# The FFN's down projection as seven products of half-size blocks

## The chip, the cores and the metric

The kernel runs on one core of one Trainium2 chip. The metric is the device time of one execution in microseconds (us). The kernel before takes 1400.53 us in the median of three runs (1400.05 to 1403.93).

## The reference, cut to what matters

One layer: a token mixer (projections, gated delta rule, pooling, output projection) and then a gated ConvFFN. All of it is float32; D is 1024, there are 1024 tokens, and D_FF is 2816, which is 22 groups of 128 channels.

```python
def conv_glu_ffn(h, w_up, conv_w, w_down):
    gate, up = jnp.split(h @ w_up, 2, axis=-1)
    return (jax.nn.silu(depthwise_conv(gate, conv_w)) * up) @ w_down

x = x + gt1 * rms_norm(yx, g_post_mix)
hx = rms_norm(x, g_pre_ffn) * (1 + sc2) + sh2
x = x + gt2 * rms_norm(conv_glu_ffn(hx, w_up, conv_ffn, w_down), g_post_ffn)
```

The change touches the last product, (1024 tokens x 2816 channels) times (2816 x 1024), and what feeds it and follows it.

## The kernel before

Every large product is made of three matmuls: each float32 operand is split into a high part (a cast on ScalarE, ACT) and a low part (a subtraction on VectorE, DVE), and high x high, high x low and low x high are summed in PSUM. A matmul is 128 x 128 weights against 512 columns.

**The up projection** (`stream_up`, `up_out`, `prep`, `stream_split`) goes by one level of Strassen's algorithm already. For each of the 22 channel groups f there are seven products of 12 matmuls each, in the order 1, 6, 2, 7, 5, 4, 3. They use three PSUM pools: `pa` and `pb` with two banks each, `pc` with four. The sums of weight blocks (tile `a`) are made on POOL; the sums of the token blocks were made once, in `stream_T`. `up_out` takes a product out of its bank; products 2, 7, 4 and 3 add onto a bank that an earlier product left, and wait until that one has been taken out (`NEEDS`). Most of that is DVE work (`graw`, `upx`), some is ACT copies (`t`).

**The gate** (`gate(f)`) follows each group: one scaling and two multiply-adds on DVE for the convolution, SiLU on ACT, a multiplication on DVE, and a store of the 128 x 1024 result into DRAM (`gd[f]`). Its buffer is row 6 or 7 of the tile `hf` (eight rows of 1024), by turns.

**The down projection** takes the groups in chunks: (0, 1), then five chunks of four. `stream_down_prep` loads each group's gate output and its rows of w_down back in halves (tile `dst`, eight buffers), and splits them into tiles `opg` and `opd`, 88 halves in all. There are 14 slots for these tiles (`SLOT`): they become free one after another as the products of the last up group (f = 21) end, and later as chunks end (`hs`). `stream_down` runs over a chunk's eight token tiles t and two column halves g: 12 matmuls into one `pc` bank (6 for the first chunk), and `down_out` copies (first chunk, ACT) or adds (DVE) the bank onto row t of `hf`.

**The last norm** is in `down_out` and `finish`, for the last chunk only: sum of squares on ACT, multiplication by a gain on POOL, then on DVE the root (Newton steps on tiny tiles) and the residual sum into `x1o`, and two stores per token tile.

All loads and stores are issued from SyncE (SP), in one queue in order. The order of instructions comes from a planner in the kernel (`Streams`, `Clock`): generators are spawned with a priority (a smaller number goes first), and `yield` of an event's name waits in the plan. On top of it the framework moves instructions forward where they find their engine free; it keeps the data dependencies and the buffers.

Of the kernel before, what the change touches and what calls it, by code (L numbers as in the profile page):

```python
# [9 lines left out]
F32 = mybir.dt.float32  # L10
# [7 lines left out]
P = 128  # L18
# [109 lines left out]
class Streams:  # L128
# [10 lines left out]
    def signal(self, name):  # L139
        self.events[name] = max(self.now, self.clock.end)  # L140
# [42 lines left out]
def kernel(ctx: ExitStack, tc: tile.TileContext, I, out):  # L183
# [68 lines left out]
    def pc(shape):  # L252
        return psC.tile(shape, F32, name="pc", tag="pc")
# [5 lines left out]
    def split_steps(dst_hi, dst_lo, src, eng=V, copy=S.copy):  # L259
        copy(dst_hi, src)  # L260
        yield (dst_hi,)
        eng.tensor_tensor(dst_lo, src, dst_hi.bitcast(F32), ALU.subtract)
        yield (dst_hi, dst_lo)
# [1203 lines left out]
    SEQ += [(f, p) for f in range(2, NF) for p in (1, 6, 2, 7, 5, 4, 3) if f > 2 or p > 2]  # L1467
    NWQ, NST = 4, 8
    half = (slice(0, 512), slice(512, 1024))
    A, wq, up, bank = {}, {}, {}, {}  # L1470
    gd = dram.tile([NF, P, T], F32, name="gd")

    def st(name):
        return fa.tile([P, 4, P], F32, name=name, tag="st", bufs=NST)

    def prep(f):

        if f:
            yield f"pre{f - 1}"
        if f == 2:  # L1480
            yield "FT"
            w = fT.tile([P, 4, 512], F32, name="a2", tag="ht", bufs=10)
            for n in range(2):
                A[f, n + 1] = w[:, n].rearrange("p (k n) -> p k n", n=P)
                dma(out=A[f, n + 1], in_=I["w_up_t"][f][:, 4 * n:4 * n + 4])
            signal("a2")
            yield (w,)
            signal("A21")
            signal("A22")
        yield "st", 4  # L1490
        src = {"11": I["w_up_t"][f][:, 0:4], "12": I["w_up_t"][f][:, 4:8],
               "21": I["w_up_t"][NF + f][:, 0:4], "22": I["w_up_t"][NF + f][:, 4:8]}
        q = {}
        for n in ("11", "21", "22", "12"):
            q[n] = st("a" + n)
            dma(out=q[n], in_=src[n])
        signal(f"pre{f}")
        if f != 2:
            A[f, 1], A[f, 2] = q["11"], q["12"]
        yield (q["11"],)  # L1500
        if f != 2:
            signal(f"A{f}1")
        yield (q["21"], q["22"])
        G.tensor_tensor(q["22"], q["21"], q["22"], ALU.add)
# [24 lines left out]
        yield (A[f, 4],)  # L1529
        signal(f"A{f}4")  # L1530
# [127 lines left out]
    def gate(f):  # L1658
        yield "TD"
        yield f"E{f}4"  # L1660
        cw = sm[:, SM_FCONV + 3 * f:SM_FCONV + 3 * f + 3]
        rw, u, sg = up[f, "g"], up[f, "u"], W["hf"][:, 6 + f % 2, :]
        V.tensor_scalar(sg, rw[:, 0:T], cw[:, 0:1], None, ALU.mult)
        yield
        V.scalar_tensor_tensor(sg, rw[:, 1:T + 1], cw[:, 1:2], sg, ALU.mult, ALU.add)
        yield
        V.scalar_tensor_tensor(sg, rw[:, 2:T + 2], cw[:, 2:3], sg, ALU.mult, ALU.add)
        yield
        S.activation(sg, sg, AF.Silu)
        yield  # L1670
        V.tensor_tensor(sg, u[:, 0:T], sg, ALU.mult)
        yield
        dma(out=gd[f], in_=sg)
        signal(f"g{f}")
        yield


    CHUNKS = [(0, 1)] + [tuple(range(f, f + 4)) for f in range(2, NF, 4)]
    SLOT = [("ha", 1), ("ha", 1), ("ht", 6), ("ht", 6), ("ha", 2), ("ha", 2), ("ht", 7), ("ht", 7), ("ht", 5), ("ht", 5),
            ("ht", 4), ("ht", 4), ("ht", 3), ("ht", 3)]  # L1680
    ops, outs = {}, {}

    def stream_down_prep():
        n = 0
        for f in range(NF):
            yield f"g{f}"
            for x in "gd":
                tag, p = SLOT[n % 14]
                if n < 14:
                    yield f"D{p}"  # L1690
                else:
                    yield "hs", 1
                n += 1
                o = (h2p if tag == "ha" else fT).tile([P, 2, T], F32R, name="op" + x, tag=tag, bufs=4 if tag == "ha" else 10)
                ops[f, x] = o
                for h in half:
                    yield "st", 1
                    w = st("dst").rearrange("p k n -> p (k n)")
                    dma(out=w, in_=gd[f][:, h] if x == "g" else I["w_down"][f * P:(f + 1) * P, h])
                    yield (w,)  # L1700
                    yield from split_steps(o[:, 0, h], o[:, 1, h], w)
                    free("st", 1)
            signal(f"d{f}")

    def stream_down():
        for fs in CHUNKS:
            last = fs[-1] == NF - 1
            for t in range(NT):
                ts = slice(t * P, (t + 1) * P)
                ps = [pc([P, 512]) for _ in range(2)]  # L1710
                for g in range(2):
                    for ff in fs:
                        yield f"d{ff}"
                        a, b = ops[ff, "g"], ops[ff, "d"]
                        for i, (y, z) in enumerate(((0, 0), (0, 1), (1, 0))):
                            TE.matmul(ps[g], lhsT=a[:, y, ts], rhs=b[:, z, half[g]], start=(ff == fs[0] and i == 0),
                                      stop=(ff == fs[-1] and i == 2))
                        yield ()
                    spawn(down_out(fs, t, g, ps[g]), 1)
            free("hs", 2 * len(fs))  # L1720

    def down_out(fs, t, g, ps):
        yield (ps,)
        if fs[0] == 0:
            yield f"g{NF - 1}"
        av = W["hf"][:, t, half[g]]
        if fs[0] == 0:
            S.copy(av, ps)
        else:
            V.tensor_tensor(av, ps, av, ALU.add)  # L1730
        yield
        if g == 0 and fs[-1] == NF - 1:
            signal(f"e{t}")
        if fs[-1] < NF - 1:
            return
        if "gg2" not in W:
            W["gg2"] = [fa.tile([P, 512], F32, name="gg2", tag="wqh", bufs=NWQ) for _ in range(2)]
            for i in range(2):
                dma(out=W["gg2"][i], in_=ggd[1, 4 * i:4 * i + 4].rearrange("k p -> (k p)").partition_broadcast(P))
        if t not in outs:  # L1740
            outs[t] = gu("x1o")[:, 0:D]
            dma(out=outs[t], in_=x1d[t])
            outs[t, "s"] = outs[t - 1, "s"] if t % 2 and t < NT - 1 else (
                small.tile([P, 2, 2], F32, name="oss", bufs=3), small.tile([P, 2], F32, name="ors", bufs=3))
        ss = outs[t, "s"][0][:, t % 2 if t < NT - 2 else 0]
        jk = fT.tile([P, 512], F32, name="t1", bufs=2)
        S.activation(jk, av, AF.Square, accum_out=ss[:, g:g + 1])
        yield
        G.tensor_tensor(av, av, W["gg2"][g], ALU.mult)
        yield  # L1750
        signal(f"o{t}{g}")
        if g:
            fin.append(t)
            if t % 2 or t == NT - 2:
                spawn(finish(tuple(fin)), 1)
                fin.clear()

    fin = []

    def finish(tiles):  # L1760

        n = len(tiles)
        yield f"o{tiles[-1]}0"
        if tiles[-1] < NT - 1:
            yield f"e{tiles[-1] + 1}"
        ss, rs = outs[tiles[0], "s"]
        sv = ss[:, 0:n, 0]
        V.tensor_tensor(sv, sv, ss[:, 0:n, 1], ALU.add)
        V.tensor_scalar(sv, sv, 1.0 / D, EPS, ALU.mult, ALU.add)
        rsqrt(rs[:, 0:n], sv, n)  # L1770
        yield
        for j, t in enumerate(tiles):
            for h in half:
                V.scalar_tensor_tensor(outs[t][:, h], W["hf"][:, t, h], rs[:, j:j + 1], outs[t][:, h], ALU.mult, ALU.add)
                dma(out=out[t * P:(t + 1) * P, h], in_=outs[t][:, h])
                yield
# [100 lines left out]
```

## Time and profile before

| | us |
|---|---|
| median of three runs | 1400.53 |
| the profiled execution | 1400.56 |
| its span, first to last instruction | 1398.8 |
| PE busy (matmuls) | 1306.9 |
| DVE busy | 932.3 |
| ACT busy | 593.1 |
| POOL busy | 326.9 |
| down projection on PE, first to last matmul | 1141.73 to 1386.32 |

A busy PE says that some matmul is in the pipeline; one matmul is recorded with 393 ns while the next starts after some 231 ns, so rates are taken from chains of many matmuls. The token mixer fills the time until about 700 us, the up projection then runs until 1141.7, and the down projection until 1386.3; what follows is the last norm.

### The profile page before, as it was taken

How to read it: one execution, taken by the hardware profiler on the slowest of the kernel's cores; microseconds unless marked ns; L12 is line 12 of the kernel's file. 1: busy time of each engine (PE TensorE's matmuls, PEld its weight loads, DVE VectorE, ACT ScalarE, POOL GpSimd, SP SyncE). 2: the span in 40 equal slices, each digit the busy share in tenths (PEclk: the TensorE clock that was granted, in tenths of full speed). 3: DMA queues.
4: the chain of work that ended last, by engine and by line, in shares of the span. 5: the costliest groups of instructions: out<-in, count | busy, mean ns of one | idle time of the engine just before them, and what ended most of it. 6: DMA issues, size and time to landing. Idle time of an engine off the chain costs nothing.

```text
span 1398.8 us, 23797 instructions
## 1 busy us (share of the span) xinstructions
PE 1306.9 (93%) x8787; PEld 1026.9 (73%) x8787; DVE 932.3 (67%) x1922; ACT 593.1 (42%) x1424; POOL 326.9 (23%) x431
## 2 busy tenths in 40 slices
PE   6788989989999899879989999999999999999996
PEld 2456767777878688658767888888888887888885
DVE  1877656657688797478798776777666693533547
ACT  3555865457575354335452333333323362210212
POOL 0552425041322300030132332333223200000024
PEclk9989999999999999999989999999999999999998
DMA  9514665545452333664213322223222364312204
GB/s 343 186 37 130 179 191 139 162 113 183 140 171 58 105 92 89 192 211 151 82 56 111 107 91 90 90 99 106 85 89 90 106 229 178 121 38 83 91 24 158
DMA packets 129460, 174.63 MB, mean 125 GB/s; under 512 B 51680, under 2 KB 64832, under 8 KB 129344
## 3 DMA queue, kind: packets, MB, share of 16 engines
q1 hardware_dynamic: 128912, 172.70, 38.1%
q8 instruction: 69, 1.13, 0.3%
q10 hardware_dynamic: 432, 0.42, 0.1%
q14 instruction: 47, 0.39, 0.1%
HBM read 135.93 MB, written 37.14 MB: 124 GB/s over the span
## 4 chain that ended last, share of the span: by engine, by line
PE 72%; DVE 13%; DMA 6%; ACT 3%; issue 3%; POOL 2%; SPq 0%; DVEq 0%; ACTq 0%; POOLq 0%
PE pc L123 30%; PE pa L123 23%; PE pb L123 19%; DMA w_m<-in_wmod 2%; DVE hf L123 1%; DMA wo_st<-in_w_out 1%; DVE rs_a L123 1%; DMA w_mod<-in_wmod 1%; DVE x L123 1%; POOL stmp L123 1%; DVE gtmp L123 1%; POOL sX L123 1%; DVE wql L123 1%; DVE yrs L123 1%; DMA dst<-in_w_down 1%
## 5 line engine op out<-in xcount | busy, mean ns | idle before, releaser
L123 PE MATMUL pc<-opd,opg 128*128 128x512 f32 x1056 | 244.4, 393 | 0.1
L123 PEld LDWEIGHTS pc<-opd,opg 128*128 128x128 f32 x1056 | 198.0, 188 | 46.4 <-ACT hf L123 0.6
L123 POOL TENSOR_TENSOR a<-a,a 128x512 f32<-128x512 f32 x88 | 131.8, 1499 | 350.8 <-DMA a<-in_w_up_t 223.5
L123 ACT CAST wqh<-a 128x512 fp32r<-128x512 f32 x132 | 81.8, 621 | 237.3 <-PE pa L123 66.3
L123 PE MATMUL pa<-h_hi,w_hi 128*128 128x512 f32 x320 | 137.8, 431 | 2.5 <-ACT jk L123 1.2
L123 PE MATMUL pa<-h_hi,w_lo 128*128 128x512 f32 x320 | 128.7, 402 | 1.6 <-DVE w_lo L123 1.6
L123 PE MATMUL pa<-h_lo,w_hi 128*128 128x512 f32 x320 | 129.3, 404 | 0.0
L123 DVE TENSOR_TENSOR hf<-pc,hf 128x512 f32<-128x512 f32 x80 | 55.0, 688 | 104.3 <-PE pc L123 104.2
L123 DVE TENSOR_TENSOR wql<-a,wqh 128x512 fp32r<-128x512 f32 x132 | 109.6, 832 | 8.4 <-ACT wqh L123 8.4
L123 ACT CAST opg<-dst 128x512 fp32r<-128x512 f32 x44 | 26.2, 621 | 142.0 <-PE pc L123 70.9
L123 POOL TENSOR_TENSOR hf<-hf,gg 128x512 f32<-128x512 f32 x16 | 22.0, 1379 | 249.0 <-ACT t L123 249.0
L123 PEld LDWEIGHTS pa<-h_hi,w_hi 128*128 128x128 f32 x320 | 60.8, 190 | 15.7 <-issue 2.6
L123 PEld LDWEIGHTS pa<-h_hi,w_lo 128*128 128x128 f32 x320 | 60.4, 189 | 13.9 <-DVE w_lo L123 1.8
L123 DVE SCALAR_TENSOR_TENSOR cv<-raw,sm,cv 128x1024 f32<-128x1024 f32 x48 | 62.2, 1297 | 11.2 <-ACT cv L123 10.7
L123 PEld LDWEIGHTS pa<-h_lo,w_hi 128*128 128x128 f32 x320 | 60.8, 190 | 9.3 <-issue 1.8
L123 DVE SCALAR_TENSOR_TENSOR hf<-graw,sm,hf 128x1024 f32<-128x1024 f32 x44 | 56.7, 1290 | 0.7
L123 DVE TENSOR_TENSOR upx<-pb,t 128x512 f32<-128x512 f32 x44 | 30.4, 690 | 38.9 <-PE pb L123 38.6
L123 ACT ACTIVATE ws<-pc,btg 128x128 f32<-128x128 f32 x80 | 26.9, 367 | 46.1 <-PE pc L123 45.7
L123 DVE TENSOR_TENSOR w_lo<-w_st,w_hi 128x512 fp32r<-128x512 f32 x40 | 28.6, 717 | 26.4 <-ACT w_hi L123 16.5
L123 PE MATMUL pc<-wo_h,mxl 128*128 128x512 f32 x112 | 44.8, 400 | 0.6 <-DVE mxl L123 0.6
L123 PE MATMUL pc<-wo_h,mxh 128*128 128x512 f32 x112 | 44.8, 401 | 0.2 <-ACT mxh L123 0.2
L123 PE MATMUL pc<-wo_l,mxh 128*128 128x512 f32 x112 | 44.5, 400 | 0.0
(378 smaller groups left out, 3236.1 us busy)
## 6 DMA issues: line engine op xcount, KB each, us to landing
a<-in_w_up_t SPq DMA_DIRECT2D x90, 256.0 KB, 2.8
w_m<-in_wmod SPq DMA_DIRECT2D x64, 256.0 KB, 3.4
gd<-hf SPq DMA_DIRECT2D x22, 512.0 KB, 2.7
dst<-gd SPq DMA_DIRECT2D x44, 256.0 KB, 3.9
dst<-in_w_down SPq DMA_DIRECT2D x44, 256.0 KB, 4.2
w_st<-in_w_in_t SPq DMA_DIRECT2D x40, 256.0 KB, 3.4
w_mod<-in_wmod SPq DMA_DIRECT2D x16, 512.0 KB, 7.5
st<-in_w_up_t SPq DMA_DIRECT2D x22, 256.0 KB, 2.8
```

Of the source, the lines that this page charges most:

```text
L123: return f(*a, **k)
```

## The change

The down projection goes by one level of Strassen's algorithm too. Tokens, channels and output columns are halved: A (tokens x channels) and B (w_down) become 2 x 2 blocks, with 11 pairs of channel groups along the sum. Channel groups are renumbered (`CH`) so that groups 2j and 2j+1 form pair j. For each pair, once its gates are done, DVE makes the four sums S1 to S4 of A's blocks (`sums_S`, four additions of 128 x 512) and the four sums T1 to T4 of B's blocks (`sums_T`, also four, after two loads of w_down), and both go to DRAM (`sd`, `td`, 1 MB each per pair). Gates now use rows 4 to 7 of `hf`, S rows 0 and 1, T rows 2 and 3. The down stage runs seven products (`DSEQ`: 1, 6, 7, 5, 4, 2, 3). Each is summed over all 11 pairs in four banks (one per token tile of a half), by turns the four of `pc` and the four of `pa` and `pb`. One operand tile `op` holds both split halves for one product and pair. The last product goes token tile by token tile. `down_out` combines the products in `hf`; the norm of a tile starts when its half is complete, for token tiles 4 to 7 after products 5 and 4.

```diff
+    CH = [f // 2 + NJ * (f % 2) for f in range(NF)]
-        rw, u, sg = up[f, "g"], up[f, "u"], W["hf"][:, 6 + f % 2, :]
+        rw, u, sg = up[f, "g"], up[f, "u"], W["hf"][:, 4 + f % 4, :]
...
+        if f % 2:
+            spawn(sums_S(f // 2), 4)
+        else:
+            spawn(sums_T(f // 2), 5)
...
+        for x, y, z, op in ((s1, a21, a22, ALU.add), (s2, s1, a11, ALU.subtract), (s3, a11, a21, ALU.subtract),
+                            (s4, a12, s2, ALU.subtract)):
+            V.tensor_tensor(x, y, z, op)
+            yield
+        dma(out=sd[j], in_=blocks(0))
...
+        for i in range(2):
+            dma(out=x[:, 2 * i:2 * i + 2], in_=I["w_down"][CH[2 * j + i] * P:(CH[2 * j + i] + 1) * P].rearrange(
+                "p (a n) -> p a n", n=512))
+        yield (x,)
+        b11, b12, b21, b22 = [x[:, i] for i in range(4)]
+        for o, y, z in ((b11, b12, b11), (b12, b22, b12), (b22, b22, b11), (b21, b21, b22)):
+            V.tensor_tensor(o, y, z, ALU.subtract)
+            yield
+        dma(out=td[j], in_=x)
...
     def stream_down_prep():
         n = 0
-        for f in range(NF):
-            yield f"g{f}"
-            for x in "gd":
...
+        for p in DSEQ:
+            for j in range(NJ):
+                a, b, ev = operands(p, j)
...
+                o = (h2p if tag == "ha" else fT).tile([P, 4, 512], F32R, name="op", tag=tag, bufs=4 if tag == "ha" else 10)
+                for i, x in enumerate((a, b)):
                     yield "st", 1
                     w = st("dst").rearrange("p k n -> p (k n)")
+                    dma(out=w, in_=x)
                     yield (w,)
+                    yield from split_steps(o[:, 2 * i], o[:, 2 * i + 1], w)
                     free("st", 1)
...
     def stream_down():
-        for fs in CHUNKS:
...
+        for i, p in enumerate(DSEQ):
+            ps = [pc([P, 512]) for _ in range(4)] if i % 2 == 0 else [x([P, 512]) for x in (pa, pa, pb, pb)]
+            def step(j, t):
+                o = ops[p, j]
+                for m, (y, z) in enumerate(((0, 0), (0, 1), (1, 0))):
+                    TE.matmul(ps[t], lhsT=o[:, y, t * P:t * P + P], rhs=o[:, 2 + z], start=(j == 0 and m == 0),
+                              stop=(j == NJ - 1 and m == 2), skip_group_check=True)
+                if j == NJ - 1:
+                    spawn(down_out(p, t, ps[t]), 1)
+            if p != DSEQ[-1]:
+                for j in range(NJ):
+                    yield f"d{p}{j}"
+                    for t in range(4):
+                        step(j, t)
...
+        c11, c12, c21, c22 = [W["hf"][:, k, h] for k in (t, 4 + t) for h in half]
+        for o, x in {1: ((c11, None),), 6: ((c12, c11),), 7: ((c21, c12),), 5: ((c22, c21), (c12, c12)), 4: ((c21, c21),),
+                     2: ((c11, c11),), 3: ((c12, c12),)}[p]:
+            if x is None:
+                S.copy(o, ps)
+            else:
+                V.tensor_tensor(o, ps, x, ALU.add)
+            yield
+        signal(f"E{p}_{t}")
+        if p in (5, 4, 2, 3):
+            spawn(down_norm(4 + t if p in (5, 4) else t, int(p in (5, 3))), 1)
```

## Rows read from the trace of the kernel before

**Rows 1.** The page's first part: busy time, share of the span, instructions.
```profile
PE 1306.9 (93%) x8787; PEld 1026.9 (73%) x8787; DVE 932.3 (67%) x1922; ACT 593.1 (42%) x1424; POOL 326.9 (23%) x431
```

**Rows 2.** Busy us by stretch: PE, PEld, DVE, ACT, POOL, granted clock, DMA share, GB/s.
```profile
757.00:1142.00 385.00, 384.35 (x1651) 310.08 (x1650) 278.73 (x332) 131.66 (x211) 111.89 (x114) 1.00 0.30 102
1142.00:1386.00 244.00, 243.85 (x1056) 197.63 (x1054) 121.84 (x212) 59.23 (x116) 18.77 (x14) 1.00 0.32 108
```

**Rows 3.** Chain of waits, up projection: start, us, what ran.
```profile
1086.02 2.81 PE pb L123 x12
1088.83 2.73 PE pa L123 x12
...
1157.40 217.84 PE pc L123 x942
```

**Rows 4.** PE's timeline across the handover and the whole down stage.
```profile
1141.50 0.40 PE L123 MATMUL pc<-B22h,wql 128*128 128x512 f32 x1
1141.73 244.59 PE L123 MATMUL pc<-opd,opg 128*128 128x512 f32 x1056
```

**Rows 5.** Groups by shape, 1142 to 1399: busy us, mean ns, idle before.
```profile
L123 DVE TENSOR_TENSOR hf<-pc,hf 128x512 f32<-128x512 f32 x80 | 55.0, 688 | 104.3 <-PE pc L123 104.2
L123 DVE TENSOR_TENSOR opd<-dst,opd 128x512 fp32r<-128x512 f32 x37 | 24.4, 683 | 3.5 <-ACT opd L123 3.4
L123 ACT CAST opd<-dst 128x512 fp32r<-128x512 f32 x36 | 21.4, 620 | 11.0 <-DMA dst<-in_w_down 10.6
```

**Rows 6.** Operand preparation alone (tile dst): DVE and ACT busy, clock, DMA share, GB/s.
```profile
1207.00:1221.00 14.00, 10.17 (x16) 9.01 (x16) 1.00 0.77 250
```

**Rows 7.** All engines in the same stretch and in the one around the handover.
```profile
1207.00:1221.00 14.00, 14.00 (x62) 11.30 (x61) 12.83 (x21) 9.01 (x16) 0.00 (x0) 1.00 0.77 250
1125.00:1157.00 32.00, 32.00 (x139) 25.70 (x137) 28.60 (x43) 23.81 (x43) 0.00 (x0) 1.00 0.83 279
```

**Rows 8.** DVE's timeline just behind the handover: the last group's gate.
```profile
1142.13 0.68 DVE L123 TENSOR_TENSOR graw<-pc,graw 128x512 f32<-128x512 f32 x1
1149.90 1.23 DVE L123 TENSOR_TENSOR hf<-upx,hf 128x1024 f32<-128x1024 f32 x1 [0.42 <-ACT hf L123]
```

**Rows 9.** Groups by shape in the up projection, 757 to 1142, DVE and POOL.
```profile
L123 DVE TENSOR_TENSOR wql<-a,wqh 128x512 fp32r<-128x512 f32 x115 | 95.4, 830 | 4.1 <-ACT wqh L123 4.1
L123 DVE TENSOR_TENSOR wql<-st,wqh 128x512 fp32r<-128x512 f32 x20 | 27.9, 1395 | 0.0
L123 POOL TENSOR_TENSOR a<-a,a 128x512 f32<-128x512 f32 x74 | 110.6, 1494 | 249.0 <-DMA a<-in_w_up_t 122.9 <-issue 80.9 <-DVE wql L123 43.8
```

**Rows 10.** POOL's and DVE's timelines where they meet, and POOL alone.
```profile
1090.01 3.59 POOL L123 TENSOR_TENSOR a<-a,a 128x512 f32<-128x512 f32 x2 [6.82 <-DMA a<-in_w_up_t]
1090.67 1.78 DVE L123 TENSOR_TENSOR wql<-st,wqh 128x512 fp32r<-128x512 f32 x1
1092.38 1.77 DVE L123 TENSOR_TENSOR wql<-a,wqh 128x512 fp32r<-128x512 f32 x1
1095.77 1.29 POOL L123 TENSOR_TENSOR a<-a,a 128x512 f32<-128x512 f32 x1 [2.10 <-DVE wql L123]
```

**Rows 11.** The up projection's stretch with the fullest DVE, and a plain one.
```profile
760.00:780.00 20.00, 19.79 (x84) 15.78 (x85) 18.53 (x22) 7.34 (x11) 4.22 (x8) 1.00 0.37 127
800.00:1100.00 300.00, 300.00 (x1290) 242.49 (x1290) 210.12 (x245) 95.48 (x153) 92.86 (x94) 1.00 0.28 94
```

**Rows 12.** DVE's take-out of a product in the up projection, with its idle time.
```profile
1080.48 0.69 DVE L123 TENSOR_TENSOR upx<-pb,t 128x512 f32<-128x512 f32 x1 [1.52 <-PE pb L123]
```

**Rows 13.** DVE's timeline at the end, in order: take-outs of the last tiles.
```profile
1383.81 0.68 DVE L123 TENSOR_TENSOR hf<-pc,hf 128x512 f32<-128x512 f32 x1
...
1390.45 0.68 DVE L123 TENSOR_TENSOR hf<-pc,hf 128x512 f32<-128x512 f32 x1
```

**Rows 14.** DMA issues: size, median us to landing.
```profile
gd<-hf SPq DMA_DIRECT2D x22, 512.0 KB, 2.7
dst<-in_w_down SPq DMA_DIRECT2D x44, 256.0 KB, 4.2
```

More of the change, by code (lines that the diff above doesn't have):

```diff
@@ L1469 @@
     half = (slice(0, 512), slice(512, 1024))
+    NJ = NF // 2
+    CH = [f // 2 + NJ * (f % 2) for f in range(NF)]
     A, wq, up, bank = {}, {}, {}, {}
     gd = dram.tile([NF, P, T], F32, name="gd")
+    sd = dram.tile([NJ, P, 4, 512], F32, name="sd")
+    td = dram.tile([NJ, P, 4, 512], F32, name="td")
     def st(name):
@@ L1484, in prep @@
                 A[f, n + 1] = w[:, n].rearrange("p (k n) -> p k n", n=P)
-                dma(out=A[f, n + 1], in_=I["w_up_t"][f][:, 4 * n:4 * n + 4])
+                dma(out=A[f, n + 1], in_=I["w_up_t"][CH[f]][:, 4 * n:4 * n + 4])
             signal("a2")
@@ L1490, in prep @@
         yield "st", 4
-        src = {"11": I["w_up_t"][f][:, 0:4], "12": I["w_up_t"][f][:, 4:8],
-               "21": I["w_up_t"][NF + f][:, 0:4], "22": I["w_up_t"][NF + f][:, 4:8]}
+        src = {"11": I["w_up_t"][CH[f]][:, 0:4], "12": I["w_up_t"][CH[f]][:, 4:8],
+               "21": I["w_up_t"][NF + CH[f]][:, 0:4], "22": I["w_up_t"][NF + CH[f]][:, 4:8]}
         q = {}
@@ L1660, in gate @@
         yield f"E{f}4"
-        cw = sm[:, SM_FCONV + 3 * f:SM_FCONV + 3 * f + 3]
-        rw, u, sg = up[f, "g"], up[f, "u"], W["hf"][:, 6 + f % 2, :]
+        cw = sm[:, SM_FCONV + 3 * CH[f]:SM_FCONV + 3 * CH[f] + 3]
+        rw, u, sg = up[f, "g"], up[f, "u"], W["hf"][:, 4 + f % 4, :]
         V.tensor_scalar(sg, rw[:, 0:T], cw[:, 0:1], None, ALU.mult)
@@ L1674, in gate @@
         signal(f"g{f}")
+        if f % 2:
+            spawn(sums_S(f // 2), 4)
+        else:
+            spawn(sums_T(f // 2), 5)
         yield
-    CHUNKS = [(0, 1)] + [tuple(range(f, f + 4)) for f in range(2, NF, 4)]
+    DSEQ = (1, 6, 7, 5, 4, 2, 3)
+    AFTER = {6: 1, 7: 6, 5: 7, 4: 5, 2: 6, 3: 5}
     SLOT = [("ha", 1), ("ha", 1), ("ht", 6), ("ht", 6), ("ha", 2), ("ha", 2), ("ht", 7), ("ht", 7), ("ht", 5), ("ht", 5),
             ("ht", 4), ("ht", 4), ("ht", 3), ("ht", 3)]
-    ops, outs = {}, {}
+    ops, outs, fin = {}, {}, []
@@ new lines, in blocks, with sums_S @@
+    def blocks(k):
+        return W["hf"][:, k:k + 2, :].rearrange("p k (a n) -> p (k a) n", n=512)
+    def sums_S(j):
+        (a11, a21), (a12, a22) = [[W["hf"][:, 4 + f % 4, h] for h in half] for f in (2 * j, 2 * j + 1)]
+        s1, s2, s3, s4 = [blocks(0)[:, i] for i in range(4)]
+        for x, y, z, op in ((s1, a21, a22, ALU.add), (s2, s1, a11, ALU.subtract), (s3, a11, a21, ALU.subtract),
[3 more added lines that the diff above has]
+        dma(out=sd[j], in_=blocks(0))
+        signal(f"S{j}d")
+        yield
@@ new lines, in sums_T @@
+    def sums_T(j):
+        x = blocks(2)
+        for i in range(2):
[7 more added lines that the diff above has]
+        dma(out=td[j], in_=x)
+        signal(f"T{j}d")
+        yield
@@ L1683, in stream_down_prep, with operands @@
+    def operands(p, j):
+        f = 2 * j + (p in (2, 4))
+        a = gd[f][:, half[p == 4]] if p in (1, 2, 4) else sd[j][:, {5: 0, 6: 1, 7: 2, 3: 3}[p]]
+        fb_ = 2 * j + (p in (2, 3))
+        b = I["w_down"][CH[fb_] * P:(CH[fb_] + 1) * P, half[p == 3]] if p in (1, 2, 3) else \
+            td[j][:, {5: 0, 7: 1, 6: 3, 4: 2}[p]]
+        return a, b, f"g{f}" if p in (1, 2, 4) else f"S{j}d"
     def stream_down_prep():
         n = 0
-        for f in range(NF):
-            yield f"g{f}"
-            for x in "gd":
-                tag, p = SLOT[n % 14]
+        for p in DSEQ:
+            for j in range(NJ):
+                a, b, ev = operands(p, j)
+                yield ev
+                yield f"T{j}d"
+                tag, q = SLOT[n % 14]
@@ L1689, in stream_down_prep @@
                 if n < 14:
-                    yield f"D{p}"
+                    yield f"D{q}"
                 else:
@@ L1693, in stream_down_prep @@
                 n += 1
-                o = (h2p if tag == "ha" else fT).tile([P, 2, T], F32R, name="op" + x, tag=tag, bufs=4 if tag == "ha" else 10)
-                ops[f, x] = o
-                for h in half:
+                o = (h2p if tag == "ha" else fT).tile([P, 4, 512], F32R, name="op", tag=tag, bufs=4 if tag == "ha" else 10)
+                ops[p, j] = o
+                for i, x in enumerate((a, b)):
                     yield "st", 1
                     w = st("dst").rearrange("p k n -> p (k n)")
-                    dma(out=w, in_=gd[f][:, h] if x == "g" else I["w_down"][f * P:(f + 1) * P, h])
+                    dma(out=w, in_=x)
@@ L1700, in stream_down_prep @@
                     yield (w,)
-                    yield from split_steps(o[:, 0, h], o[:, 1, h], w)
+                    yield from split_steps(o[:, 2 * i], o[:, 2 * i + 1], w)
                     free("st", 1)
-            signal(f"d{f}")
+                signal(f"d{p}{j}")
     def stream_down():
-        for fs in CHUNKS:
[L1707 to L1717, printed above, removed]
-                        yield ()
-                    spawn(down_out(fs, t, g, ps[g]), 1)
-            free("hs", 2 * len(fs))
@@ L1722, in down_out @@
-    def down_out(fs, t, g, ps):
-        yield (ps,)
[L1724 to L1728, printed above, removed]
-        else:
[L1730 to L1735, printed above, removed]
+        for i, p in enumerate(DSEQ):
[12 more added lines that the diff above has]
+                        step(j, t)
+                        yield ()
+                    free("hs", 1)
+            else:
+                for j in range(NJ):
+                    yield f"d{p}{j}"
+                for t in range(4):
+                    for j in range(NJ):
+                        step(j, t)
+                        yield ()
@@ new lines, in down_out @@
+    def down_out(p, t, ps):
+        yield (ps,)
+        if p == 1:
+            yield f"S{NJ - 1}d"
+            yield f"T{NJ - 1}d"
+        else:
+            yield f"E{AFTER[p]}_{t}"
+        c11, c12, c21, c22 = [W["hf"][:, k, h] for k in (t, 4 + t) for h in half]
[3 more added lines that the diff above has]
+                S.copy(o, ps)
+            else:
+                V.tensor_tensor(o, ps, x, ALU.add)
+            yield
+        signal(f"E{p}_{t}")
+        if p in (5, 4, 2, 3):
+            spawn(down_norm(4 + t if p in (5, 4) else t, int(p in (5, 3))), 1)
@@ L1736, in down_out, with down_norm @@
+    def down_norm(t, g):
         if "gg2" not in W:
@@ L1739, in down_out @@
                 dma(out=W["gg2"][i], in_=ggd[1, 4 * i:4 * i + 4].rearrange("k p -> (k p)").partition_broadcast(P))
-        if t not in outs:
+        if (t, "s") not in outs:
+            outs[t, "s"] = small.tile([P, 2], F32, name="oss", bufs=8)
             outs[t] = gu("x1o")[:, 0:D]
             dma(out=outs[t], in_=x1d[t])
-            outs[t, "s"] = outs[t - 1, "s"] if t % 2 and t < NT - 1 else (
-                small.tile([P, 2, 2], F32, name="oss", bufs=3), small.tile([P, 2], F32, name="ors", bufs=3))
-        ss = outs[t, "s"][0][:, t % 2 if t < NT - 2 else 0]
+        av = W["hf"][:, t, half[g]]
         jk = fT.tile([P, 512], F32, name="t1", bufs=2)
-        S.activation(jk, av, AF.Square, accum_out=ss[:, g:g + 1])
+        S.activation(jk, av, AF.Square, accum_out=outs[t, "s"][:, g:g + 1])
         yield
@@ L1750, in down_out @@
         yield
-        signal(f"o{t}{g}")
-        if g:
+        done["o", t] = done.get(("o", t), 0) + 1
+        if done["o", t] == 2:
             fin.append(t)
-            if t % 2 or t == NT - 2:
+            if t % 2 or t == 2:
                 spawn(finish(tuple(fin)), 1)
                 fin.clear()
-    fin = []
     def finish(tiles):
         n = len(tiles)
[L1763 to L1770, printed above, removed]
+        ss, rs = [small.tile([P, 2], F32, name=x, bufs=3) for x in ("ofs", "ors")]
+        for j, t in enumerate(tiles):
+            V.tensor_tensor(ss[:, j:j + 1], outs[t, "s"][:, 0:1], outs[t, "s"][:, 1:2], ALU.add)
+        V.tensor_scalar(ss[:, 0:n], ss[:, 0:n], 1.0 / D, EPS, ALU.mult, ALU.add)
+        rsqrt(rs[:, 0:n], ss[:, 0:n], n)
         yield
```

## The prediction

> **What bounds the kernel now.** I read the page's busy line first [rows 1]: PE has 1306.9 us of a span of 1398.8. That is an average, so the next view is busy time by stretch [rows 2]. In the up projection (757 to 1142 us) PE has 384.35 of 385, in the down projection 243.85 of 244, at a granted clock of 1.00 (2.4 GHz); DVE is busy 72% of the first and 50% of the second. The chain of waits [rows 3] stays on PE there: 942 down matmuls follow one another for 217.84 us. PE's timeline [rows 4] shows no seam: the last up matmul starts at 1141.50, the first down matmul at 1141.73, and 1056 of them take 244.59 us, 0.2316 us each. So in the two stages that the change touches a matmul less is 0.23 us less, as long as nothing else takes PE's place. The third part is the tail behind 1386.32.
>
> **Matmuls.** Before: 22 groups x 8 token tiles x 2 halves x 3 = 1056. After: 7 products x 11 pairs x 4 tiles x 3 = 924. 132 fewer x 0.2316 = 30.6 us less; 924 take 214.0 us. The new loop changes bank after 3 matmuls instead of 12, which no row shows. The nearest rows are the up products, 12 matmuls in one bank: 2.73 us (0.2275 each) and 2.81 us (0.2342 each) [rows 3]. 924 at these prices are 210.2 and 216.4 us, so the saving lies between 28.2 and 34.4 us; I take 0.2316, the price with the same kind of operand tiles. If all of 0.2316 over 0.2275 were the price of a change of bank (0.0041 x 12 = 0.05 us), 308 changes instead of 88 would cost 11 us; the 2.81 us product, without any change of bank, speaks against that.
>
> **Preparing operands.** Before 88 halves are loaded, cast and subtracted, now 77 tiles x 2 = 154. At 0.683 us (DVE) and 0.620 us (ACT) [rows 5] that is 105 and 95 us, beside 28 additions out of PSUM (19 us, where 80 were 55). DVE has some 140 us of work with the norm, in 214. DMA has 154 x 0.262 MB = 40.4 MB, or 189 GB/s. PE eats one tile in 12 x 0.2316 = 2.78 us. What the engines can do is seen where a chunk ends and eight slots come free at once: 16 halves, which are eight of the new tiles, are loaded (a load lands in 4.2 us, [rows 14]) and go through both engines in 14 us [rows 6], 1.75 us per tile, at 250 GB/s, while PE stays at 14.00 of 14 [rows 7]. That is within 2.78. These preparations run beside the take-outs, not behind them, up to 14 tiles ahead, so I cost the stage at nothing. That cover is PE's 39 us of prepared work; without it a tile's casts and two subtractions would stand on the path at every end of a product (rivals).
>
> **The handover.** Product 1 needs four `pc` banks; the last up product holds one until its addition, 1142.13 to 1142.81 [rows 8]. The fourth bank is first written nine matmuls in, at 1143.8. No wait. The last gate ends at 1151.1 [rows 8]; four sums (2.7 us) and a store (2.7 us, [rows 14]) end about 1157. Product 1's copies on ACT now wait for that store and the last T store, since they overwrite those rows of `hf`; they come at 1141.7 + 11 x 2.78 = 1172, and the casts behind them on ACT are covered by the tiles ahead. DVE and ACT are busy 28.60 and 23.81 of 32 us around the handover [rows 7], and preparing 14 tiles there is what they do already.
>
> **The sums in the up projection.** 8 additions per pair x 11 = 88 more on DVE, with both inputs in SBUF. The nearest row is the weight split: 0.68 us alone, but 1.78 and 1.77 us when POOL runs its own sums, where two POOL sums also take 3.59 us instead of 2 x 1.29 [rows 10]. So 60 us when none meets POOL. DVE is idle 385 - 278.7 = 106 us there [rows 2], so it rises from 72% to 88%. For the upper bound: POOL runs 74 sums [rows 9]; the splits show 115 x (0.830 - 0.683) + 20 x (1.395 - 0.683) = 31 us of meeting already, 28 meetings at 1.1 us. If each of the other 46 met one of the new sums, 60 + 51 = 111 us would be added: DVE just full, 5 us over. What does PE lose on the way? PE needs a take-out (0.69 us) within the next product's 2.8 us, and DVE is idle 1.5 us before many of them [rows 12], so one 0.68 us addition ahead does no harm. At 93% DVE, from 760 to 780, PE lost 0.21 us of 20; at 70%, from 800 to 1100, nothing [rows 11]. Over 385 us that is 0 to 4 us; I take 2.0 for 88%.
>
> What the trace shows here, a POOL sum and a DVE addition each running longer when they meet, the Trainium skill's page "SBUF — State Buffer", section "Who interferes with whom", states as an exclusive lock: a DVE instruction with two SBUF inputs and a GpSimd one that reads SBUF do not share, the second one waits for the first. It speaks against putting these sums on DVE; its result is the third rival.
>
> SP gets four more DMAs per pair (two loads, two stores, 3.1 MB, 89 GB/s over the stage, on top of 102 at share 0.30). A store of S waits on SP for its sums, and up-weight loads queue behind it; POOL's sums, their first user, run far ahead (POOL idles 249 us between its sums [rows 9]), so I cost that at nothing; without this cover it would be the few us of a burst, once per pair.
>
> **The tail.** PE ends at 1386.32 [rows 4], but the last take-out starts at 1390.45 [rows 13], behind the previous tile's root and residual sum on DVE. From there 8.35 us lead to 1398.8. In the new last product a token tile has 33 matmuls, 7.6 us, and a tile's way from take-out to its last residual sum is about 6.7 us (1383.81 to 1390.53), so DVE is free when PE ends: 4.1 us less. Bounds: 0 (the same order again) to 4.1. The norms of tiles 4 to 7 move, with their POOL multiplications, loads and stores, beside products 4 and 2, where POOL is idle and PE busy.
>
> **Sum.** Against the profiled execution, 1400.56 us (its span and 1.76 us around it; the median is 1400.53): 1400.56 - 30.6 - 4.1 + 2.0 = 1367.9 us.
>
> **Rivals.**
> - Static order in the down stage or late take-outs in the up stage cost some of it. If at each of six ends of products PE finds no prepared tile (take-out 0.69, two subtractions 1.37, 0.2 for the signals), 6 x 2.3 = 13.8 us: 1381.7. Or if four sums bunch ahead of a take-out in each pair, some 1.3 us x 11 = 14 us. For: DVE runs in order and the sums come right behind the gate, where the long splits lie. Against: the preparations between take-outs at 1207 to 1221. Chance 0.18, 1374 to 1384.
> - The matmul gets dearer and eats the gain, so the change doesn't do what it counts: at 244.59 / 924 = 0.265 us nothing is left of the 30.6, 1398.5. Only the bank change every 3 matmuls could do it. Against: 0.2275 to 0.2342 in all rows, whatever bank. Chance 0.04.
> - Slower: DVE becomes the bound of the up projection because the sums meet POOL. It decides from a mean price of a sum of 106 / 88 = 1.20 us, and the gain of 34.7 is gone at (106 + 34.7) / 88 = 1.60 us; at 1.78 us for all 88, 51 us over the idle time, it gives 1365.9 + 51 = 1417 us. For: 1.78 us per meeting. Against: POOL's 74 sums cannot meet more than once each by the rows, and then DVE is only 5 us over. Chance 0.05.
>
> By the lock as that page has it, a sum waits for a whole POOL sum, 0.68 + 1.29 = 1.97 us at most, which for all 88 would give about 1433 us; the measured 1.78 says that it waits for most of one.
>
> **How the numbers follow.** Forecast 1367.9 with chance 0.70: its own range is 1362 (34.4 saved on matmuls, no loss) to 1377 (28.2 saved, no gain in the tail, 4 us lost). 0.18 for the first rival, 0.04 and 0.05 for the next two, and 0.03 for better than 1362. A range that leaves out no more than 2 in 10 takes in most of the first rival: 1361 to 1383. A measurement can tell about 0.3% (4.2 us) from no change. Faster by more: 0.70 + 0.18 + 0.03 = 0.91; within: 0.04; slower: 0.05.
>
> **What would show it.** Right: 924 down matmuls in one unbroken run of 212 to 217 us; PE at 99% or more from 757 to 1142 with DVE near 88%; preparations some 10 tiles ahead; the last take-out within 0.1 us of PE's end. Wrong: waits of PE for `graw` or `upx` of more than 5 us in all (first rival, up); PE idle behind each product (first rival, down); a matmul above 0.24 us; sums with a mean above 1.2 us and the down stage starting well behind 1145.

## The result, and the profile after

The changed kernel takes 1377.27 us in the median of four runs (1374.41 to 1380.53); its time is 0.9827 of that of before, 95% interval 0.9806 to 0.9847. The profiled execution took 1374.41 us, against 1367.9 forecast and a range of 1361 to 1383. It has a span of 1372.7 us.

First comes busy time by stretch, with the columns of [rows 2]: the up projection and its two parts.

```profile
757.00:1142.00 385.00, 377.03 (x1611) 301.64 (x1610) 325.81 (x397) 125.09 (x202) 116.29 (x114) 1.00 0.48 176
757.00:975.00 218.00, 210.03 (x892) 166.45 (x891) 194.56 (x239) 67.02 (x107) 68.98 (x67) 1.00 0.57 213
975.00:1142.00 167.00, 167.00 (x720) 135.19 (x720) 131.24 (x159) 58.07 (x95) 47.31 (x47) 1.00 0.35 127
```

The same for the instructions on the operand tiles alone (PE, PEld, DVE, ACT, clock, DMA share, GB/s), in the down stage from where it runs without a break:

```profile
1156.38:1364.16 207.78, 207.77 (x909) 170.56 (x909) 92.25 (x136) 77.83 (x134) 1.00 0.63 212
```

PE loses 8.0 us of the 385, where it lost 0.65 before. All of it is lost ahead of 975, where DVE is busy 89%. The down stage is as full as before. PE's timeline around the handover:

```profile
1145.91 2.21 PE L123 MATMUL pc<-op 128*128 128x512 f32 x9
1147.96 0.40 PE L123 MATMUL pb<-T4h,wqh 128*128 128x512 f32 x1
...
1153.58 1.53 PE L123 MATMUL pc<-op 128*128 128x512 f32 x6
1156.38 26.97 PE L123 MATMUL pc<-op 128*128 128x512 f32 x117 [1.27 <-DVE graw L123]
```

The waits of PE in the up projection, 757 to 1142 (who waited for whom: us in all, times, longest):

```profile
PE pb L123 <- DVE upx L123: 6.2, 5, 1.8
PE pb L123 <- DVE graw L123: 0.6, 1, 0.6
```

The stretch from the first to the last up matmul of one kind is a measure of the up projection that start times ahead of it don't touch; a window's busy time hides that a matmul behind a wait is itself longer. I take the matmuls of product 6 on the tile `T2h`. Their row in the kernel before (count, ns min/median/max, first and last start), and then in the changed kernel:

```profile
L123 PE MATMUL pb<-T2h,wqh x88: 388/394/628, 718.0 to 1127.1; 128*128 128x512 f32 x88
```

```profile
L123 PE MATMUL pb<-T2h,wqh x88: 392/394/628, 717.9 to 1136.9; 128*128 128x512 f32 x88
```

That is 409.1 us before and 419.0 after, and gives the account of the profiled executions:

| term, us | forecast | measured |
|---|---|---|
| down matmuls: 244.59 [rows 4], now 2.05 + 1.53 + 207.78 = 211.4 | -30.6 | -33.2 |
| up projection: 409.1, now 419.0 | +2.0 | +9.9 |
| wait of PE at the handover | 0 | +1.3 |
| tail: 1398.8 - 1386.32, now 1372.7 - 1364.16 | -4.1 | -3.9 |
| sum | -32.7 | -25.9 |

The whole difference is 1400.56 - 1374.41 = 26.15 us; 0.2 is left over. So the question is the up projection: where do nearly 8 us go that the forecast did not have? Five waits at the first matmul of product 4 make up the 6.2 us. Here is DVE's timeline ahead of one of the longest:

```profile
799.93 1.23 DVE L123 TENSOR_TENSOR hf<-upx,hf 128x1024 f32<-128x1024 f32 x1
801.08 0.69 DVE L123 TENSOR_TENSOR wql<-st,wqh 128x512 fp32r<-128x512 f32 x1
801.68 0.68 DVE L123 TENSOR_TENSOR hf<-hf 128x512 f32<-128x512 f32 x1
802.28 1.81 DVE L123 TENSOR_TENSOR wql<-a,wqh 128x512 fp32r<-128x512 f32 x1
804.01 2.98 DVE L123 TENSOR_TENSOR hf<-hf 128x512 f32<-128x512 f32 x3
806.91 0.68 DVE L123 TENSOR_TENSOR upx<-pb,t 128x512 f32<-128x512 f32 x1
```

And POOL's in the same stretch:

```profile
802.25 2.99 POOL L123 TENSOR_TENSOR a<-a,a 128x512 f32<-128x512 f32 x2 [7.77 <-DMA a<-in_w_up_t]
```

The gate of an odd group has just ended, POOL runs two sums of up weights, and four of the new sums (`hf<-hf`) stand ahead of `upx<-pb`, the take-out of product 7. PE needs that bank for product 4 and waits 1.30 us, until 807.74. Four of the five waits look like this. The earliest, at 766, does not: there two instructions of the gate itself ran for 2.39 and 2.31 us beside POOL. From the gate's last multiplication to the take-out it is 7.0 to 7.3 us at these four waits. Where it is 6.5 us or less, which it is everywhere else behind 790, PE does not wait. In the kernel before it is 4.9 us from 796 to 1114:

```profile
1089.54 1.22 DVE L123 TENSOR_TENSOR hf<-upx,hf 128x1024 f32<-128x1024 f32 x1
...
1094.40 0.69 DVE L123 TENSOR_TENSOR upx<-pb,t 128x512 f32<-128x512 f32 x1 [0.26 <-PE pb L123]
```

The new sums as a group in 757 to 1142 (busy us, mean ns, idle before), then, by tile, all of them with their spread (ns min/median/max), and the stores of T:

```profile
L123 DVE TENSOR_TENSOR hf<-hf 128x512 f32<-128x512 f32 x80 | 76.2, 961 | 2.2 <-DMA hf<-in_w_down 1.7
```

```profile
L123 DVE TENSOR_TENSOR hf<-hf x89: 677/687/1794, 714.8 to 1167.0; 128x512 f32<-128x512 f32 x89
```

```profile
L123 SPq DMA_DIRECT2D td<-hf x11: 326/327/327, 748.1 to 971.7; - x11
```

Their mean is 0.96 us and not 0.68, and the last of the eleven T stores goes out at 971.7: T needs nothing from the gates, and its 44 sums were carried forward into the part ahead of 975. Three causes offered themselves: T crowds the first half; DVE simply has too much to do; or DVE meets POOL.

### The profile page after: what moved, and what is told of

It reads as the page before. It is cut to its first block, busy times and chain, and to the rows that moved or that the text cites. A ratio compares the mean times of both kernels' runs of the same rounds, so it can differ in the third digit from the quotient of the medians.

```text
span 1372.7 us, 23957 instructions
## 1 busy us (share of the span) xinstructions
PE 1276.5 (93%) x8655; PEld 1003.6 (73%) x8655; DVE 999.7 (73%) x2027; ACT 624.3 (45%) x1478; POOL 333.8 (24%) x431
## 5 line engine op out<-in xcount | busy, mean ns | idle before, releaser
L123 POOL TENSOR_TENSOR a<-a,a 128x512 f32<-128x512 f32 x88 | 137.9, 1568 | 354.2 <-DMA a<-in_w_up_t 130.1
L123 DVE TENSOR_TENSOR op<-dst,op 128x512 fp32r<-128x512 f32 x154 | 104.1, 717 | 62.2 <-ACT op L123 61.9
L123 ACT CAST op<-dst 128x512 fp32r<-128x512 f32 x154 | 89.8, 620 | 99.1 <-PE pc L123 34.2
L123 PE MATMUL pc<-op 128*128 128x512 f32 x528 | 121.7, 391 | 1.3 <-DVE graw L123 1.3
L123 PEld LDWEIGHTS pc<-op 128*128 128x128 f32 x528 | 99.1, 188 | 23.2 <-DVE graw L123 1.7
L123 DVE TENSOR_TENSOR wql<-a,wqh 128x512 fp32r<-128x512 f32 x132 | 101.3, 769 | 19.0 <-ACT wqh L123 18.6
L123 DVE TENSOR_TENSOR hf<-hf 128x512 f32<-128x512 f32 x89 | 82.4, 933 | 2.2 <-DMA hf<-in_w_down 1.7
L123 PE MATMUL pa<-op 128*128 128x512 f32 x198 | 50.6, 391 | 0.0
L123 PE MATMUL pb<-op 128*128 128x512 f32 x198 | 50.4, 390 | 0.0
```

The source lines that it names most:

```text
L123: return f(*a, **k)
```

## The experiments

All times are ratios to the kernel before, with their 95% intervals. Each ratio comes from runs of both kernels on one chip, which is not the same chip for all rows. "Up" is the stretch from the first to the last T2h matmul as above, from one profile of each run. Two runs leave the up projection as they found it, the kernel before with two banks by turns and the last product by pairs, and each repeats the stretch of its kernel to 0.1 us.

| kernel | ratio | up, us |
|---|---|---|
| before | 1 | 409.1 |
| before, two banks by turns | 1.0003 [0.9989, 1.0018] | 409.0 |
| after | 0.9827 [0.9806, 0.9847] | 419.0 |
| no T | 0.9765 [0.9739, 0.9791] | 410.2 |
| T moved, not summed | 0.9774 [0.9747, 0.9800] | 412.6 |
| T in turn with S | 0.9810 [0.9788, 0.9833] | 418.1 |
| T on POOL | 0.9972 [0.9955, 0.9989] | 442.2 |
| no sums on POOL | 0.9663 [0.9636, 0.9691] | 407.5 |
| last product by pairs | 0.9870 [0.9843, 0.9897] | 418.9 |
| scaling on ACT, pa first | 0.9817 [0.9787, 0.9847] | 419.8 |
| T from PSUM | 0.9734 [0.9710, 0.9759] | 412.2 |
| T and S from PSUM | 0.9750 [0.9722, 0.9778] | 411.5 |

**No T.** `sums_T` only signals, and products 4 to 7 read plain blocks of w_down.

```diff
-        b11, b12, b21, b22 = [x[:, i] for i in range(4)]
-        for o, y, z in ((b11, b12, b11), ...):
-            V.tensor_tensor(o, y, z, ALU.subtract)
-            yield
-        dma(out=td[j], in_=x)
...
-            td[j][:, {5: 0, 7: 1, 6: 3, 4: 2}[p]]
+            I["w_down"][CH[2 * j + p % 2] * P:(CH[2 * j + p % 2] + 1) * P, half[p // 6]]
```

> Leaves out all T sums with their loads and stores (products 4 to 7 read plain blocks of w_down instead). Bunching theory (the T sums are carried forward into 742 to 972 us, two pairs' worth in the time of one, and crowd take-outs there): PE loses at most 1 us of 757 to 1142 instead of 8.0, and the time falls by 6 to 8 us against the changed kernel, ratio to before about 0.977 to 0.979. Rival, S sums and the gate's new rows cost as much as the T sums: PE still loses 4 us and the gain is 4 us or less.

The up projection is 8.8 us shorter than after's, 1.1 above before's: with T gone nearly all of the loss is gone, and the S sums and the gate's new rows alone cost almost nothing. They cost so little although they meet POOL: the 41 S sums of 757 to 1142 take 1.14 us on average. With three of them ahead of the take-out it is 6.5 us behind the gate's multiplication, still in time. What T would cost without S, no run shows.

**T moved, not summed.** The two loads and the store stay, the four subtractions go.

> Leaves out the 44 T additions but keeps their loads (22 of 512 KB) and stores (11 of 1 MB). If the additions on DVE make the loss: like the run without T, PE loses at most 1 us of 757 to 1142, 6 to 8 us faster than the changed kernel. If the traffic or SP's queue makes it: PE still loses 6 to 8 us, time as the changed kernel.

412.6 us: 2.4 more than without the traffic, 6.4 less than with the sums. Loads, stores and SP's queue together cost a quarter of the loss (no run takes them apart), the additions on DVE the rest.

**T in turn with S.** One line: T uses the buffer of S, so that T can't run ahead. T and S of one pair share the buffer with no order between them, so part of T is overwritten before it is stored; count, shape and place of the instructions are those of the whole.

```diff
-        x = blocks(2)
+        x = blocks(0)
```

> T is made in the buffer of S, so pair j's T waits for pair j-1's S to be stored: the same 88 additions, but T's last store near 1110 instead of 972 us. Bunching theory: PE loses at most 2 us of 757 to 1142, 5 to 7 us faster than the changed kernel, ratio to before about 0.978. Rival, it is the amount of DVE work wherever it lies: PE loses 7 to 8 us again, only later, ratio 0.983.

T's stores now leave some 40 us apart, the last at 1145, and the up projection still takes 418.1 us. PE's waits at the same place, the first matmul of product 4, are more and mostly shorter: ten, with 5.6 us in all, from 757 to 1142, the longest 2.3 us. Three of those from 840 on:

```profile
851.48 0.47 PE L123 MATMUL pb<-T4h,wqh 128*128 128x512 f32 x1 [0.54 <-DVE upx L123]
...
990.58 0.47 PE L123 MATMUL pb<-T4h,wqh 128*128 128x512 f32 x1 [0.35 <-DVE upx L123]
...
1109.77 0.47 PE L123 MATMUL pb<-T4h,wqh 128*128 128x512 f32 x1 [0.45 <-DVE upx L123]
```

I took this for the end of the theory of bunching: with T's pairs spread out, the loss is the same but for 0.9 us. It doesn't show that, since the run brings a delay of its own. The loads into the shared buffer come late, and DVE stands for them, 18.7 us in all from 757 to 1142, at 2.2 to 2.8 us ahead of most odd gates behind 840:

```profile
977.32 0.69 DVE L123 TENSOR_TENSOR hf<-hf 128x512 f32<-128x512 f32 x1 [2.44 <-DMA hf<-in_w_down]
```

The wait at 990 above follows on this one: the gate is late, and only one sum stands between its multiplication and the take-out. So the run leaves bunching open.

**T on POOL.** `V.tensor_tensor` in `sums_T` becomes `G.tensor_tensor`.

> The 44 T additions go to POOL instead of DVE. If the load of DVE makes PE's loss: DVE returns to about 80% of 757 to 975, PE loses at most 3 us there instead of 8.0, ratio to before 0.978 to 0.980. Rival, the meetings of POOL and DVE make it: POOL runs 118 sums instead of 74, the splits and S sums meet them more often, and PE loses 8 us or more.

DVE is relieved of 44 additions, and the loss is three times as large: 442.2 us, and nearly the whole gain of the change is gone. DVE's other work is longer now; here are the S sums, and the gate's multiply-adds, which took 1290 ns in the same stretch before and 1333 in the changed kernel:

```profile
L123 DVE TENSOR_TENSOR hf<-hf 128x512 f32<-128x512 f32 x37 | 41.3, 1120 | 0.3
L123 DVE SCALAR_TENSOR_TENSOR hf<-graw,sm,hf 128x1024 f32<-128x1024 f32 x40 | 58.6, 1466 | 0.6
```

Not all of the 33 us come from that. PE's waits for take-outs (`graw` and `upx`) from 757 to 1142 are 18.3 us, against 6.8 in the changed kernel. POOL, with more to do, makes the up weights' sums later: DVE stands idle 37.6 us for the casts behind them, against 16.6. And with PE idle for 21.6 of the 218 us ahead of 975, the mean granted clock there is 0.95, between its two levels of 2.4 and 1.2 GHz, where it was 1.00; by an estimate from that row this costs some 0.05 x 218 = 11 us:

```profile
757.00:975.00 218.00, 196.41 (x794) 154.69 (x793) 170.79 (x180) 58.96 (x96) 118.75 (x100) 0.95 0.57 200
```

DVE is busy 78% of this stretch, less than in the changed kernel, and PE loses more. So DVE's load isn't the cause either.

**No sums on POOL.** POOL's four sums per group in `prep` are left out (the up products take plain weight blocks); all 88 new sums on DVE stay.

> Leaves out POOL's 88 sums of the up weights (the products take plain blocks); all 88 new sums on DVE stay. If the meetings with POOL lengthen what stands ahead of product 7's take-out: no DVE addition above 0.75 us, PE loses at most 2 us of 757 to 975 instead of 8.0, ratio about 0.978. Rival, the additions alone are too many at that place: DVE still loses PE 5 us or more.

The up projection takes 407.5 us, less than before's, with every new sum in place. In 757 to 975 PE loses nothing (columns as in [rows 2]), and not one addition is above 0.70 us:

```profile
757.00:975.00 218.00, 218.00 (x939) 176.22 (x938) 173.23 (x246) 69.77 (x111) 1.46 (x22) 1.00 0.62 218
```

```profile
L123 DVE TENSOR_TENSOR hf<-hf x89: 678/684/696, 705.7 to 1146.7; 128x512 f32<-128x512 f32 x89
```

The same instructions stand in the same order ahead of the same take-out as in the timeline at 800, each at its own price, and it is 4.95 us from the multiplication to the take-out instead of 6.98:

```profile
786.20 1.22 DVE L123 TENSOR_TENSOR hf<-upx,hf 128x1024 f32<-128x1024 f32 x1
...
788.73 0.69 DVE L123 TENSOR_TENSOR wql<-a,wqh 128x512 fp32r<-128x512 f32 x1
789.34 1.89 DVE L123 TENSOR_TENSOR hf<-hf 128x512 f32<-128x512 f32 x3
791.15 0.69 DVE L123 TENSOR_TENSOR upx<-pb,t 128x512 f32<-128x512 f32 x1
```

So the number of sums at that place is not enough to make PE wait; and the meetings are not either, since the kernel before and the run without T have them there. It takes four sums, T's bunched with S's, and the meetings together. The meetings of DVE and POOL are the cause in this sense, and the bunching counts through them. POOL's sums being gone from the first groups' preparation too, this kernel begins the up projection 8.5 us earlier, so its ratio isn't that of the meetings alone; the stretch is.

**T from PSUM.** ACT copies two blocks of w_down into free `pc` banks, and three of the four T additions take one input from there.

```diff
+        p11, p22 = [pc([P, 512]) for _ in range(2)]
+        for o, y in ((p11, b11), (p22, b22)):
+            S.copy(o, y)
+            yield
-        for o, y, z in ((b11, b12, b11), (b12, b22, b12), (b22, b22, b11), (b21, b21, b22)):
+        for o, y, z in ((b11, b12, p11), (b12, p22, b12), (b22, p22, b11), (b21, b21, b22)):
```

> ACT copies two of the four w_down blocks of a pair into free pc banks, and three of the four T additions read one input from there: same count and place, 22 more ACT copies. Take-outs out of PSUM never ran above 0.694 us in any run, additions of two SBUF tiles ran to 1.79. If the meetings with POOL are the cause: the T additions' mean falls, PE loses 2 to 4 us of 757 to 975 instead of 8.0, ratio 0.979 to 0.981. Rival, the pc banks held by T delay the up products, or the number of additions counts: PE loses 8 us or more.

412.2 us, and a ratio of 0.9734, clear of the changed kernel's: the complete computation, faster than both kernels. Of the profiled execution's 9.2 us below the changed kernel's, 6.8 are the up projection, 1.3 the handover, where PE no longer waits, and 1.0 an earlier start of the up projection; the two ratios differ by 13 us, and the rest of that is not placed. The T additions with an input in PSUM never ran above 0.693 us (the first group also holds 12 take-outs of down products); those with two SBUF inputs, S's above all, still reach 1.785:

```profile
L123 DVE TENSOR_TENSOR hf<-pc,hf x34: 676/682/693, 769.3 to 1355.0; 128x512 f32<-128x512 f32 x34
L123 DVE TENSOR_TENSOR hf<-hf,pc x11: 672/674/678, 768.1 to 1136.1; 128x512 f32<-128x512 f32 x11
L123 DVE TENSOR_TENSOR hf<-hf x56: 678/687/1785, 713.7 to 1157.4; 128x512 f32<-128x512 f32 x56
```

But price is not all that changed. Waiting for banks also moved T's additions: they now come behind the take-out of product 7, and only S sums, three at most, stand ahead of it, 6.6 us or less behind the multiplication. The S sums meet POOL as before. So the 6.8 us can be owed to the new place as much as to the price, and no run takes the two apart. That DVE's load doesn't count comes out once more beside the run with the scaling on ACT, further down. DVE is busy 86% of 757 to 975 in both, and PE loses 2.8 us here and 8.7 there. Here, and then there:

```profile
757.00:975.00 218.00, 215.21 (x921) 172.48 (x920) 186.77 (x230) 76.76 (x124) 64.68 (x69) 1.00 0.51 182
757.00:975.00 218.00, 209.31 (x889) 165.62 (x888) 186.59 (x228) 79.20 (x118) 66.96 (x67) 1.00 0.60 215
```

**T and S from PSUM.** The same for S, with copies of a21 and a11.

> The same for the S additions (44 more ACT copies in all). If the meetings with POOL are the cause: mean of the 88 additions below 0.80 us instead of 0.96, PE loses at most 3 us of 757 to 1142, ratio 0.977 to 0.980, the fastest complete version. Rival, four pc banks in use by sums hold up the up products: PE waits for banks and loses 8 us or more.

411.5 us; the ratio's interval overlaps that of T alone. Here sums with an input in PSUM do stand ahead of the take-out, and from 802 to 1115 it is 4.9 to 6.0 us behind the multiplication. But the run before had left PE only 0.8 us of waits there: S had almost nothing to give back, as the run without T says.

**Scaling on ACT, pa first.** `V.tensor_scalar(sg, rw[:, 0:T], cw[:, 0:1], ...)` becomes `S.activation(sg, rw[:, 0:T], AF.Copy, scale=cw[:, 0:1])`, and the products start on `pa` and `pb`.

> The gate's first scaling goes from DVE to ACT (22 x 0.74 us less on DVE), and the seven products start on the banks pa and pb instead of pc. The load theory says: PE loses 4 to 6 us of 757 to 975 instead of 8.0. The wait of 1.3 us for graw behind the handover goes. Together 3 to 5 us faster than the changed kernel, ratio 0.979 to 0.981. Rival, only what stands between the gate's end and product 7's take-out counts: the loss stays near 8 us, and only the 1.3 us are won.

419.8 us: DVE has 16 us less to do and PE loses as much as ever. Part of the relief is taken back, since DVE now waits 10.2 us for the gate's work on ACT. But the scaling never stood between the gate's end and the take-out, and the four sums still do. The handover's 1.3 us are won: from 1130 to 1170 PE waits for nothing. That is too little for the ratio to show beside the up projection's 0.8 us more.

**Last product by pairs.** `if p != DSEQ[-1]` becomes `if True`.

> The last product runs pair by pair over four banks like the others, so all four tiles end together. The tail's term says: the time behind PE's end grows from 8.5 us to 15 to 20 us, ratio 0.988 to 0.991. Rival, the tail is carried by the stores: at most 3 us more. Of the matmul's price: if taking four banks by turns makes it cheaper, its 132 matmuls take 30.1 us instead of 30.4.

PE ends at 1365.69 and the span at 1381.7: 16.0 us of tail instead of 8.5. The 132 matmuls of the last product, by pairs over four banks, and then in the changed kernel, tile by tile:

```profile
1335.41 30.28 PE L123 MATMUL pc<-op 128*128 128x512 f32 x132
```

```profile
1333.59 30.57 PE L123 MATMUL pc<-op 128*128 128x512 f32 x132
```

**The kernel before, two banks by turns.** The loops over `ff` and `g` in `stream_down` change places.

> The kernel before, with its down loop turned: the two column halves by turns, so that the bank changes after 3 matmuls instead of 12; all else equal. If the change of bank is what made the down matmul cheaper (0.2278 instead of 0.2316 us): 1056 matmuls in 239.5 to 241.5 us instead of 244.6, ratio 0.997 to 0.998. If it is the operand tile (both halves in one tile): 244.6 us as before, ratio 1.000.

The ratio is 1.0003, 0.9989 to 1.0018. The matmuls take 14.73 us for 63, then 228.38 for 993, 0.2300 each. That lies between the two expectations: this order wins some of the difference, and not all that the new loop has.

## Why the prediction was right, and which term was off

- **Matmuls.** The mechanism and the size held: 132 fewer, PE without a gap from 1156 to 1364. The bounds, 0.2275 to 0.2342 us, hold the measured 211.4 / 924 = 0.2288. I feared that a change of bank every three matmuls could cost up to 0.05 us; it costs nothing, and the stage is 2.6 us shorter than forecast. (The kernel before changes its bank 96 times and not 88, since its first chunk has six matmuls to a bank; nothing hangs on it.)
- **Preparing operands: nothing.** Held. DVE is busy 92 us with operands in 208 and PE waits for none, with 212 GB/s at a DMA share of 0.63.
- **The handover: no wait.** Wrong by 1.3 us, for two reasons. I counted nine matmuls between the start of the down stage and the first use of the fourth bank. Nine down matmuls had been carried forward, into a place between two up products, so that only six were left behind the last up matmul. And the last addition to `graw`, which starts 0.6 us behind the start of the last up matmul in [rows 4] and [rows 8], came 2.3 us behind it. The last up matmul on PE, and then DVE:

```profile
1153.34 0.39 PE L123 MATMUL pc<-B22h,wql 128*128 128x512 f32 x1
```

```profile
1154.42 1.30 DVE L123 TENSOR_TENSOR op<-dst,op 128x512 fp32r<-128x512 f32 x2 [1.95 <-ACT op L123]
1155.64 0.69 DVE L123 TENSOR_TENSOR graw<-pc,graw 128x512 f32<-128x512 f32 x1
```

  DVE had stood idle for a cast of ACT and then did two operand splits first. By these rows six matmuls, until about 1155.0, would have covered an addition in time, and nine, until about 1155.7, would not have covered this one; that is an estimate. I had preparation and handover each at nothing, and not what the one does to the other.
- **The sums in the up projection: +2.0.** This is the term that was mis-sized: it measured 9.9. I made two steps. The bound on the price of a sum, from [rows 9] and [rows 10], took in what came, a mean of 0.96 us. Even that is not a net price: POOL's 74 sums met the new sums in place of the splits. The 80 sums took 21.8 us more than 0.68 us each, and the splits, 95.4 + 27.9 us in [rows 9], 16.8 us less:

```profile
L123 DVE TENSOR_TENSOR wql<-a,wqh 128x512 fp32r<-128x512 f32 x115 | 87.3, 759 | 17.0 <-ACT wqh L123 16.6
L123 DVE TENSOR_TENSOR wql<-st,wqh 128x512 fp32r<-128x512 f32 x20 | 19.2, 958 | 0.0
```

  The step that failed is the one from DVE's busy share to PE's loss: I read 0.21 us in 20 at 93% DVE [rows 11] and took less for 88%. The run with the scaling on ACT has less on DVE and the same loss, and the run without POOL's sums has 88 sums more than before on DVE and no loss. What counts most is one place: behind the gate's last multiplication POOL runs two sums, DVE's splits there take 1.78 us each already in most groups [rows 10], and the take-out of product 7 follows with 2 us to spare. That is room for three sums with two meetings; where four of S's and T's sums stood there, behind the gate of an odd group, the rest went straight into PE's time.
- **The tail: -4.1.** Held, -3.9: the last take-out starts at 1364.19, 0.03 us behind PE's end. The run by pairs shows the price of the other order, 7.5 us.
- **Rivals.** The time, 1377.27, lies in the first rival's band (1374 to 1384), by its second form, sums bunched ahead of a take-out. Its sign came too: 6.8 us of waits for `upx` and `graw`, where I had named 5, and PE at 98% and not 99. The forecast's own range ends at 1400.56 - 28.2 + 4 = 1376.4, put down as 1377, so the time lies just outside it. The wider range holds it because it took in this rival, to which I had given 0.18, and because the matmuls gave 2.6 us more than I had taken. That part is luck. The third rival, DVE meeting POOL, had half of the mechanism but not the size: I set its point at DVE being full, while it costs PE long before that, by 8 us and not 51. Additions with an input in PSUM ran 0.693 us at most, those with two SBUF inputs up to 1.785. The page of the Trainium skill that I weighed the rival by, "SBUF — State Buffer", section "Who interferes with whom", agrees with the runs on both: it has the lock for two SBUF inputs, and says that an instruction with at most one SBUF input, outside DVE's two-port modes, doesn't contend.

What stays open: why the up projection of the best version is still 2 to 3 us above before's. Its waits are single ones of 1 us or less, and the T traffic alone cost 2.4. Open too is how much of what T from PSUM won comes from the additions' price and how much from their place.

## What to carry to other kernels

A busy share doesn't price added work: find the place in each round where a take-out or another deadline follows, and ask what the new instruction does there, beside which engine. Elementwise work on DVE with both inputs in SBUF, next to POOL sums, can take 2.6 times its time and lengthens POOL's sums too; an input in a free PSUM bank, copied there by an ACT with time to spare, keeps it at its price. Here that, together with the later place that the additions got by it, took the ratio from 0.9827 to 0.9734. And work that depends on nothing around it need not run where the program puts it, so a cover counted in instructions (nine matmuls) holds only if the order can't move them and if what they cover comes on time.

## What the runs showed that I had not expected

Matmuls are a little cheaper in the order in which successive groups of three go to different banks. In the same kernel, with the same operand tiles, 132 matmuls take 30.07 us with the bank changing every three over four banks, and 30.42 with 33 in a row in one bank (0.2278 and 0.2305 us); the run by pairs and the kernel before with two banks by turns (0.2300, against 0.2316) point the same way. Two rows of the chain of waits, after:

```profile
1213.47 30.07 PE pc L123 x132
...
1333.75 30.42 PE pc L123 x132
```

The bank need not be the reason: in each of these orders the operand tiles also change less often, after 12 matmuls instead of 3, or in the kernel before after 6, and no run keeps one and changes the other. The remaining step from 0.2316 to 0.2305 goes with the new operand tile, which holds weights and moving columns together, and with 33 matmuls in a row instead of 12; no run took that apart.
